# Low parts of the down projections' activation operands: from subtractions on VectorE and GpSimd to adding transfers

## Chip, cores and metric

One core of a Trainium2 chip. The metric is the device time of one execution in microseconds (us); of several executions the median is taken.

## What is computed

Two decoder layers over 1024 tokens of 1024 features, in float32. Each layer is attention (latent attention in layer 0, differential attention in layer 1) and then a SwiGLU block of 2816 hidden columns; a norm ends the program.

```python
def _swiglu(h, w_gate_up, w_down):
    gu = h @ w_gate_up
    return (jax.nn.silu(gu[..., :D_FF]) * gu[..., D_FF:]) @ w_down
...
        h = h + _swiglu(_rmsnorm(h, ffn_norm[l]), ffn_w_gate_up[l], ffn_w_down[l])
    return _rmsnorm(h, final_norm)
```

The change touches the operands of the product with `w_down`, once in each layer.

## The kernel before

**Numbers.** TensorE multiplies float32r operands. A float32 value is split into a high part (rounded to float32r) and a low part (what is left), and a product takes three matmuls: high by high, low by high, high by low (`product`, L1264). `split` (L412) makes such a pair: ScalarE writes the high part with an activation, then VectorE, or GpSimd where `sub` says so, subtracts it from the source and writes the low part.

**The down projection.** `block_tail` (L1126) holds what follows attention. Its first stage (`up`, L1339) makes the gated hidden columns in 11 pairs and writes them to HBM (`act_d`); its second stage (`down`, L1406, and `down_last`, L1440) multiplies them by `w_down` in Strassen's form with seven products. The operands of the seven products come from `stage(p)` (L1529): it loads four tiles of a pair p from `act_d` into tiles named `stg` and makes four sums of them on VectorE; `place(xs, p, i)` (L1550) then splits the staged tile of form i into `xh` and `xl`, 128x512 each. There are 11 pairs of 7 forms in 2 layers, 154 calls of `place`. Forms 0, 1, 3 and 5 are subtracted on VectorE (88 instructions), forms 2, 4 and 6 on GpSimd (66).

```python
    GROUPS = ((0, 1), (2, 3, 4), (5, 6, 7), (8, 9, 10))
    SLOTS = (0, 1, 2, 3, 0, 1, 2, 3, 0, 1, 2)
```

The 11 pairs are multiplied in four groups. For a group, `down` runs over n = 0 to 3, and for each n over the seven products; a product of a group of three pairs is nine matmuls. There are four places (slots) for operands. While group g is multiplied, `prepare` stages and places those pairs of group g + 1 whose slots the group does not use. The other pairs (one of group 1, two each of groups 2 and 3) can be placed only at n = 3, form i right after product i has read the old tile; we call this a group switch. The 14 operands of group 0 are placed while the last pair of `up` runs and right after it.

In the second stage VectorE also subtracts weight columns from each other (`wr`), makes their low parts (`wl`; the high parts `wh` come from ScalarE), and adds each product from PSUM (`pa`, `pb`, `pc`) to the sums `h`. GpSimd has little but the 33 subtractions of each layer.

**The order.** The instructions of a stage are recorded, and a planner (`Plan`) sets their order once, when the program is built: it takes, with costs from `cost` (L294), what can start first on each engine. Each engine then runs its instructions in that order. All recorded instructions are issued in one line, so the profile shows L287 for nearly all of them; tiles tell them apart. SP issues all DMAs. GpSimd issues none.

Of the kernel before, what the change touches and what calls it, by code (L numbers as in the profile page):

```python
# [14 lines left out]
AF = mybir.ActivationFunctionType  # L15
ALU = mybir.AluOpType
# [176 lines left out]
class Plan:  # L193
# [100 lines left out]
    def cost(self, engine, name, n, dtype, psum, accum, size):  # L294

        if engine == "tensor":
            if name == "transpose":
                return 0.107, self.HOP
            return n * (1 if dtype == F32R else 6 if n <= 64 else 8) / 2400, self.HOP
        if engine == "scalar":  # L300
            return (0.05 if psum else 0.09) + n / 1200 + 0.19 * accum, self.HOP
        if engine == "vector":
            return 0.067 + n / 960 + 0.063 * (name == "scalar_tensor_tensor" and not psum), self.HOP
        if engine == "gpsimd":
            return (0.245 + n / 1200 if name == "tensor_scalar" else 0.15 + n / 475), self.HOP
        return max(0.45, size / 360e3), 2.2
# [64 lines left out]
def trunk(ctx: ExitStack, tc: tile.TileContext, A: dict):  # L371
    nc = Plan(tc)
# [33 lines left out]
    def f32(ap):  # L406
        return ap.bitcast(F32)
# [4 lines left out]
    def split(dst_hi, dst_lo, src, scale=1.0, sub=None):  # L412
        nc.scalar.activation(dst_hi, src, AF.Copy, scale=scale)
        if isinstance(scale, float) and scale == 1.0:
            (sub or nc.vector).tensor_tensor(dst_lo, src, f32(dst_hi), ALU.subtract)
        else:
            nc.vector.scalar_tensor_tensor(dst_lo, src, scale, f32(dst_hi), ALU.mult, ALU.subtract)

    def mm3(ps, parts):
        n = len(parts)  # L420
        for i, (lh, ll, rh, rl) in enumerate(parts):
            nc.tensor.matmul(ps, lhsT=lh, rhs=rh, start=i == 0, stop=False)
            nc.tensor.matmul(ps, lhsT=lh, rhs=rl, start=False, stop=False)
            nc.tensor.matmul(ps, lhsT=ll, rhs=rh, start=False, stop=i == n - 1)
# [117 lines left out]
    with tc.using_default_side("right"):  # L542
# [9 lines left out]
                t=("z6", "z7", "z8", "z9", "t", "t"), xh=[q + "h" for q in spare], xl=[q + "l" for q in spare],  # L552
# [76 lines left out]
    for k in range(KT):  # L629
        xt[k] = load_x(0, k)  # L630
        raw = wa_p.tile([P, NA * P], F32, name="war", tag="war", bufs=3)
        wh = wa_p.tile([P, NA * P], F32R, name=f"wah{k}", tag=f"wah{k}")
        wl = wa_p.tile([P, NA * P], F32R, name=f"wal{k}", tag=f"wal{k}")
        cuts = (0, 2 * P, 4 * P, NA * P) if k == 0 else (0, NA * P)
        if k == 0:
            nc.sync.dma_start(out=gains, in_=A["gains"])
        for a, b in zip(cuts, cuts[1:]):
            nc.sync.dma_start(out=raw[:, a:b], in_=A["wa"][k, :, a:b])
            split(wh[:, a:b], wl[:, a:b], raw[:, a:b], sub=nc.vector if k < 2 else nc.gpsimd)
        wa_h.append(wh)  # L640
        wa_l.append(wl)
# [4 lines left out]
    def compressed(f, acc, r):  # L646
# [17 lines left out]
        for norm, (which, _, lo_n, n_t, dst_h, dst_l) in zip(norms, kinds):  # L664
            yield
            rr = norm.spread()
            for n in range(n_t):
                t = tmpa.tile([P, HF], F32, name="cn", tag="t")
                nc.vector.scalar_tensor_tensor(t, raws[lo_n + n], gain(which, n), rr, ALU.mult, ALU.mult)
                split(dst_h[n][f], dst_l[n][f], t)  # L670
# [3 lines left out]
        nc.vector.tensor_tensor(m2[0:64], kraw[64:128], cs[64:128, tok], ALU.mult)  # L674
        nc.vector.tensor_tensor(m1[0:64], m1[0:64], m2[0:64], ALU.add)
        split(krh[0:64, tok], krl[0:64, tok], m1[0:64])
        for t in (krh, krl):
            move(t[64:128, tok], t[0:64, tok])
# [447 lines left out]
    def block_tail(layer, half, resid, last, side_work=None, ahead=None, meanwhile=None):  # L1126
# [11 lines left out]
        def zpool(place):  # L1138
            return z1 if int(place[1:]) < 10 else z2
# [11 lines left out]
        def dtile(i, s):  # L1151
            return xtile(*DOWN.get((i, s), (i, s)))
# [374 lines left out]
        staged = {}  # L1527
# [11 lines left out]
        def prepare(xs, free, pairs):  # L1539

            for p in free:
                yield from stage(p)
                for i in range(7):
                    place(xs, p, i)
                    if i % 2:
                        yield
            for p in pairs:
                yield from stage(p)

        def place(xs, p, i):  # L1550
            t = dtile(i, SLOTS[p])
            split(*t, staged[p][i], sub=nc.vector if i in (0, 1, 3, 5) else nc.gpsimd)
            xs[i].append(t)


# [34 lines left out]
        for p in range(NJ // 2):  # L1590
            if p == 2 and side_work is not None:
                side_work(z1)
            if p == CUT[layer]:
                quarter_operands(1, whole, nc.vector)
            for m, i in ups[p]:
                if p < NJ // 2 - 1:
                    continue
                if (m, i) == (1, 1):
                    for _ in stage(0):
                        pass  # L1600
                    place(xs, 0, 0), place(xs, 0, 1)
                if (m, i) == (0, 4):
                    for _ in stage(1):
                        pass
                if m == 1 and i >= 2:
                    place(xs, 0, i)
# [3 lines left out]
        for g in range(len(GROUPS) - 1):  # L1610
# [5 lines left out]
            for n in range(4):  # L1616
                i = 0
# [362 lines left out]
```

## Time and profile before

| | |
|---|---|
| median of 3 runs | 2520.44 us (2517.12 to 2521.76) |
| the profiled execution | 2517.07 us, of which 2515.0 us are the span of the trace |
| granted TensorE clock, mean | 0.977 of full speed |
| TensorE busy (PE) | 2335.8 us, 93% |
| VectorE busy (DVE) | 1929.2 us, 77% |
| ScalarE busy (ACT) | 1164.3 us, 46% |
| GpSimd busy (POOL) | 1125.1 us, 45% |

PE is TensorE's matmul, PEld its weight load, DVE VectorE, ACT ScalarE, POOL GpSimd, SP the engine that issues DMAs. Busy shares are means over stages that have different limits, so the argument goes by stretches of the span. The `stg` tiles are read by `place` from 933 to 1172 us (layer 0) and from 2204 to 2440 us (layer 1). A matmul's end is modelled and overlaps the next one's start, so how fast TensorE runs is read from starts and counts, not from busy time.

### The profile page before, as it was taken

What the parts mean: (1) busy time and instruction counts of PE and PEld (TensorE: products, weight loads), DVE (VectorE), ACT (ScalarE), POOL (GpSimd) and SP (SyncE); (2) the same over time, 40 slices, a digit from 0 to 9 for tenths busy, and PEclk for the clock granted to TensorE, in tenths of its full rate; (3) what the DMA queues carried; (4) which work ended last, traced back from release to release, by engine and by line L of the source; (5) the groups of instructions that cost most, each with busy time, mean ns of one, the idle gap of its engine ahead of it and who ended that gap; (6) DMA issues with size and microseconds to landing.
All of it is one profiled execution on the core that took longest, in us unless ns stands there. A gap on an engine that the chain in (4) does not pass through costs nothing. (4 is left out here: it accounts for less than half of the span.)

```text
span 2515.0 us, 38090 instructions
## 1 busy us (share of the span) xinstructions
PE 2335.8 (93%) x12744; PEld 1996.4 (79%) x12744; DVE 1929.2 (77%) x3685; ACT 1164.3 (46%) x2319; POOL 1125.1 (45%) x979
## 2 busy tenths in 40 slices
PE   8689999999899998999999999989989999988997
PEld 6579988778788886777788888878768888876777
DVE  6575555387887789999678677676598787789997
ACT  4246555244444444344355555554344444454442
POOL 2145652163555554123377674444264555542212
PEclk9899999999999998999999999999999999999999
DMA  5156665566332235332266663373744232244322
GB/s 182 22 158 203 197 199 177 163 214 202 111 92 72 84 104 179 92 105 92 87 201 198 207 196 113 106 233 125 251 142 154 79 93 72 85 147 149 103 66 73
DMA packets 204691, 347.41 MB, mean 138 GB/s; under 512 B 26832, under 2 KB 59856, under 8 KB 204496
## 3 DMA queue, kind: packets, MB, share of 16 engines
q1 hardware_dynamic: 204496, 344.99, 43.8%
q8 instruction: 101, 1.65, 0.3%
q14 instruction: 94, 0.77, 0.1%
HBM read 240.94 MB, written 95.04 MB: 134 GB/s over the span
## 5 line engine op out<-in xcount | busy, mean ns | idle before, releaser
L287 ACT ACTIVATE wh<-wr 128x512 fp32r<-128x512 f32 (+2 forms) x530 | 287.5, 550 | 450.1 <-PE pb L287 137.7
L287 DVE TENSOR_TENSOR wl<-wr,wh 128x512 fp32r<-128x512 f32 (+2 forms) x530 | 396.0, 761 | 38.6 <-ACT wh L287 38.0
L287 PE MATMUL pa<-xh,wh 128*128 128x512 f32 (+1 forms) x850 | 339.6, 401 | 35.9 <-DVE h L287 16.2
L287 PE MATMUL pa<-xh,wl 128*128 128x512 f32 (+1 forms) x850 | 337.3, 398 | 18.4 <-DVE wl L287 17.1
L287 PE MATMUL pa<-xl,wh 128*128 128x512 f32 (+1 forms) x850 | 336.6, 396 | 4.0 <-DVE xl L287 4.0
L287 PE MATMUL pb<-xh,wh 128*128 128x256 f32 (+1 forms) x976 | 293.7, 304 | 23.4 <-DVE s L287 17.4
L287 PE MATMUL pb<-xl,wh 128*128 128x256 f32 (+1 forms) x976 | 293.0, 301 | 0.0
L287 PE MATMUL pb<-xh,wl 128*128 128x256 f32 (+1 forms) x976 | 291.8, 301 | 0.0
L287 POOL TENSOR_TENSOR wr<-wr 128x512 f32<-128x512 f32 x128 | 179.6, 1403 | 172.6 <-DMA wr<-wgu 84.3
L287 POOL TENSOR_TENSOR xl<-stg,xh 128x512 fp32r<-128x512 f32 x66 | 110.9, 1698 | 305.3 <-ACT xh L287 159.0
L287 PEld LDWEIGHTS pa<-xh,wh 128*128 128x128 f32 x850 | 163.0, 192 | 77.5 <-DVE h L287 14.6
L287 PEld LDWEIGHTS pb<-xh,wh 128*128 128x128 f32 x976 | 187.6, 193 | 46.2 <-DVE s L287 26.6
L287 PEld LDWEIGHTS pa<-xh,wl 128*128 128x128 f32 x850 | 162.1, 191 | 57.0 <-DVE wl L287 24.8
L287 PEld LDWEIGHTS pb<-xl,wh 128*128 128x128 f32 x976 | 188.5, 193 | 13.7
L287 PEld LDWEIGHTS pb<-xh,wl 128*128 128x128 f32 x976 | 188.0, 193 | 6.0 <-DVE wl L287 0.5
L287 PEld LDWEIGHTS pa<-xl,wh 128*128 128x128 f32 x850 | 163.0, 192 | 34.4 <-DVE xl L287 5.7
L287 POOL TENSOR_SCALAR p<-p,tot 128x640 f32<-128x640 f32 (+7 forms) x128 | 98.9, 774 | 180.6 <-DVE tot L287 114.0
L287 ACT ACTIVATE p<-sc,nmax 128x128 f32<-128x128 f32 (+7 forms) x192 | 141.8, 740 | 77.6 <-DVE nmax L287 45.3
L287 POOL TENSOR_TENSOR qt<-wr 128x256 f32<-128x256 f32 x120 | 102.8, 876 | 124.8 <-DVE wl L287 107.2
L287 DVE TENSOR_TENSOR s<-s,pb 128x256 f32<-128x256 f32 (+1 forms) x278 | 115.6, 426 | 39.5 <-PE pb L287 36.6
L287 PE MATMUL pc<-xh,wh 128*128 128x512 f32 x352 | 139.1, 398 | 4.5 <-DVE h L287 4.3
L287 PE MATMUL pc<-xl,wh 128*128 128x512 f32 x352 | 138.9, 395 | 2.5 <-DVE xl L287 2.5
(295 smaller groups left out, 6491.2 us busy)
## 6 DMA issues: line engine op xcount, KB each, us to landing
wr<-wgu SPq DMA_DIRECT2D x142, 256.0 KB, 3.2
act_d<-s SPq DMA_DIRECT2D x88, 256.0 KB, 2.5
stg<-act_d SPq DMA_DIRECT2D x88, 256.0 KB, 2.9
wr<-wd SPq DMA_DIRECT2D x96, 192.0 KB, 2.4
pb<-wgu SPq DMA_DIRECT2D x60, 256.0 KB, 4.0
preh<-ph SPq DMA_DIRECT2D x58, 256.0 KB, 3.0
prel<-pl SPq DMA_DIRECT2D x58, 256.0 KB, 2.8
wh<-preh SPq DMA_DIRECT2D x58, 256.0 KB, 4.8
```

Source lines behind the costliest of these rows:

```text
L287: return getattr(getattr(self.nc, engine), name)(*map(put, args), **{k: put(a) for k, a in kw.items()})
```

## The change

`place` no longer calls `split`. For all seven forms ScalarE writes the high part as before, then writes the negated rounded source, which is the negated high part, into the low tile, and a DMA issued from GpSimd adds the staged tile to the low tile in place. The subtractions on VectorE and GpSimd are gone. The planner gets a cost for such a DMA.

```diff
@@ -301,6 +301,8 @@
             return (0.05 if psum else 0.09) + n / 1200 + 0.19 * accum, self.HOP
         if engine == "vector":
             return 0.067 + n / 960 + 0.063 * (name == "scalar_tensor_tensor" and not psum), self.HOP
+        if name == "dma_start" and engine == "gpsimd":
+            return 0.9, 3.8
         if engine == "gpsimd":
             return (0.245 + n / 1200 if name == "tensor_scalar" else 0.15 + n / 475), self.HOP
         return max(0.45, size / 360e3), 2.2
@@ -416,6 +418,12 @@
         else:
             nc.vector.scalar_tensor_tensor(dst_lo, src, scale, f32(dst_hi), ALU.mult, ALU.subtract)
 
+    def low_by_transfer(dst_hi, dst_lo, src):
+
+        nc.scalar.activation(dst_hi, src, AF.Copy)
+        nc.scalar.activation(dst_lo, src, AF.Copy, scale=-1.0)
+        nc.gpsimd.dma_start(out=f32(dst_lo), in_=src, accum_op=ALU.add)
+
     def mm3(ps, parts):
         n = len(parts)
         for i, (lh, ll, rh, rl) in enumerate(parts):
@@ -1549,7 +1557,10 @@
 
         def place(xs, p, i):
             t = dtile(i, SLOTS[p])
-            split(*t, staged[p][i], sub=nc.vector if i in (0, 1, 3, 5) else nc.gpsimd)
+            if i in (0, 1, 2, 3, 4, 5, 6):
+                low_by_transfer(*t, staged[p][i])
+            else:
+                split(*t, staged[p][i], sub=nc.vector if i in (0, 1, 3, 5) else nc.gpsimd)
             xs[i].append(t)
 
 
```

The planner's order moves with it, at three places that matter here. The first is GpSimd where `up` ends and the second stage begins (`wr` and `qt` are sums of the last gate and up weights, `xl<-stg` the low parts of the operands). Before:

```order
L287 TENSOR_TENSOR qt<-wr,qt 128x256
L287 TENSOR_TENSOR wr<-wr 128x512 x4
L287 TENSOR_TENSOR xl<-stg,xh 128x512
L287 TENSOR_TENSOR qt<-wr 128x256 x2
L287 TENSOR_TENSOR qt<-wr,qt 128x256
L287 TENSOR_TENSOR xl<-stg,xh 128x512
L287 TENSOR_TENSOR qt<-wr,qt 128x256
L287 TENSOR_TENSOR xl<-stg,xh 128x512 x27
```

Now:

```order
L287 DMA xl<-stg 128x512
L287 TENSOR_TENSOR wr<-wr 128x512 x2
L287 DMA xl<-stg 128x512
L287 TENSOR_TENSOR wr<-wr 128x512
L287 DMA xl<-stg 128x512
L287 TENSOR_TENSOR wr<-wr 128x512
L287 DMA xl<-stg 128x512
L287 TENSOR_TENSOR qt<-wr 128x256 x2
L287 DMA xl<-stg 128x512
L287 TENSOR_TENSOR qt<-wr,qt 128x256
L287 DMA xl<-stg 128x512
L287 TENSOR_TENSOR qt<-wr,qt 128x256
```

Six issues of transfers now stand ahead of the last `qt`, where two subtractions stood, and three more `wr` are behind a transfer.

The second is VectorE at a group switch of layer 0 (`h` takes the sums from PSUM, `wr` and `wl` are weight columns of the next n). Before:

```order
L287 TENSOR_TENSOR h<-h,pb 128x512
L287 TENSOR_TENSOR xl<-stg,xh 128x512
L287 TENSOR_TENSOR wl<-wr,wh 128x384
L287 TENSOR_TENSOR h<-h,pa 128x512
L287 TENSOR_TENSOR wr<-wr 128x384
L287 TENSOR_TENSOR xl<-stg,xh 128x512 x2
L287 TENSOR_TENSOR h<-h,pc 128x512
L287 TENSOR_TENSOR xl<-stg,xh 128x512
L287 TENSOR_TENSOR wl<-wr,wh 128x384
L287 TENSOR_TENSOR h<-h,pa 128x512
```

Now:

```order
L287 TENSOR_TENSOR h<-h,pb 128x512
L287 TENSOR_TENSOR h<-h,pa 128x512
L287 TENSOR_TENSOR h<-h,pc 128x512
L287 TENSOR_TENSOR h<-h,pa 128x512
L287 TENSOR_TENSOR h<-h,pc 128x512
L287 TENSOR_TENSOR h<-h,pa 128x512 x2
L287 TENSOR_TENSOR wl<-wr,wh 128x384 x3
```

No operand work stands between two additions from PSUM; the weights' low parts `wl` come later than the sums.

The third is ScalarE at the same switch (`wh` are high parts of weight columns). Before:

```order
L287 ACTIVATE xh<-stg 128x512 x3
L287 ACTIVATE wh<-wr 128x384
L287 ACTIVATE xh<-stg 128x512
L287 ACTIVATE wh<-wr 128x384
L287 ACTIVATE xh<-stg 128x512 x3
L287 ACTIVATE wh<-wr 128x384
L287 ACTIVATE xh<-stg 128x512 x3
```

Now (the pattern of the last two rows goes on, until 27 activations have run without a `wh`):

```order
L287 ACTIVATE wh<-wr 128x384 x22
L287 ACTIVATE xl<-stg 128x512
L287 ACTIVATE xh<-stg 128x512 x2
L287 ACTIVATE xl<-stg 128x512 x2
L287 ACTIVATE xh<-stg 128x512 x2
L287 ACTIVATE xl<-stg 128x512
L287 ACTIVATE xh<-stg 128x512
```

The high and negated parts of the operands have moved together, and the weights' high parts ahead of them and behind them.

## Rows read from the trace of the kernel before

**Rows 1.** The page: busy us, share and count of engines; VectorE in 40 slices.
```profile
PE 2335.8 (93%) x12744; PEld 1996.4 (79%) x12744; DVE 1929.2 (77%) x3685; ACT 1164.3 (46%) x2319; POOL 1125.1 (45%) x979
...
DVE  6575555387887789999678677676598787789997
```
**Rows 2.** Stretches of the second stages: PE, PEld, DVE, ACT, POOL busy; clock, DMA share, GB/s.
```profile
980.00:1010.00 30.00, 24.88 (x96) 18.75 (x95) 30.00 (x56) 12.26 (x25) 9.75 (x6) 0.89 0.70 226
1010.00:1190.00 180.00, 166.29 (x709) 132.42 (x708) 176.71 (x293) 75.96 (x149) 45.38 (x30) 0.99 0.32 97
...
2260.00:2290.00 30.00, 24.66 (x90) 17.80 (x89) 29.97 (x54) 11.43 (x25) 9.82 (x6) 0.89 0.67 221
2290.00:2450.00 160.00, 147.42 (x630) 118.01 (x629) 155.58 (x261) 67.21 (x132) 33.90 (x21) 0.99 0.30 91
```
**Rows 3.** Matmuls in time order, 14 without a wait: start, us.
```profile
1050.01 0.39 PE L287 MATMUL pb<-xh,wh 128*128 128x512 f32 x1
...
1052.96 0.39 PE L287 MATMUL pc<-xh,wh 128*128 128x512 f32 x1
```
**Rows 4.** Whom PE waited for, 980 to 1190: us in total, times, longest.
```profile
PE pa L287 <- DVE h L287: 9.0, 7, 2.3
PE pc L287 <- DVE h L287: 3.6, 2, 3.1
PE pa L287 <- DVE wl L287: 3.2, 1, 3.2
```
**Rows 5.** VectorE's groups, 980 to 1190: busy us, mean ns.
```profile
L287 DVE TENSOR_TENSOR wl<-wr,wh 128x384 fp32r<-128x384 f32 x76 | 47.1, 634 | 0.0
...
L287 DVE TENSOR_TENSOR xl<-stg,xh 128x512 fp32r<-128x512 f32 x34 | 30.9, 921 | 0.0
L287 DVE TENSOR_TENSOR wr<-wr 128x384 f32<-128x384 f32 x47 | 29.5, 636 | 0.0
L287 DVE TENSOR_TENSOR stg<-stg 128x512 f32<-128x512 f32 x36 | 28.6, 801 | 0.0
```
**Rows 6.** VectorE and GpSimd in time order, 1136 to 1165: start, us.
```profile
1139.27 0.55 DVE L287 TENSOR_TENSOR wl<-wr,wh 128x384 fp32r<-128x384 f32 x1
...
1143.86 1.66 DVE L287 TENSOR_TENSOR wl<-wr,wh 128x384 fp32r<-128x384 f32 x1
...
1143.67 3.00 POOL L287 TENSOR_TENSOR xl<-stg,xh 128x512 fp32r<-128x512 f32 x2 [38.08 <-ACT xh L287]
```
**Rows 7.** The tile stg, its readers: duration ns min/median/max; last, its loads' time to landing.
```profile
L287 ACT ACTIVATE xh<-stg x154: 612/628/637, 933.2 to 2437.4; 128x512 fp32r<-128x512 f32 x154
L287 SPq DMA_DIRECT2D stg<-act_d x88: 319/326/1054, 685.0 to 2388.5; - x88
L287 DVE TENSOR_TENSOR xl<-stg,xh x88: 677/686/1786, 934.6 to 2437.5; 128x512 fp32r<-128x512 f32 x88
L287 DVE TENSOR_TENSOR stg<-stg x88: 678/683/1792, 947.9 to 2401.2; 128x512 f32<-128x512 f32 x88
L287 POOL TENSOR_TENSOR xl<-stg,xh x66: 1267/1614/4807, 954.1 to 2439.3; 128x512 fp32r<-128x512 f32 x66
...
DMA to landing us min/median/max: 2.3/2.9/5.0
```
**Rows 8.** In time order where the second stage of layer 0 begins: start, us, idle before.
```profile
954.06 4.81 POOL L287 TENSOR_TENSOR xl<-stg,xh 128x512 fp32r<-128x512 f32 x1 [6.92 <-ACT xh L287]
958.83 1.44 POOL L287 TENSOR_TENSOR qt<-wr 128x256 f32<-128x256 f32 x2
...
960.30 0.63 ACT L287 ACTIVATE wh<-qt 128x512 fp32r<-128x512 f32 x1 [3.74 <-POOL qt L287]
...
967.07 0.58 PE L287 MATMUL pb<-xh,wh 128*128 128x256 f32 x1 [6.15 <-DVE s L287]
```
**Rows 9.** A DMA from SBUF to SBUF (128 KB each): us to landing.
```profile
qa<-qa SPq DMA_DIRECT2D x32, 128.0 KB, 2.7
```

## The prediction, made before the changed kernel ran

> **What bounds the kernel now.** I read the page first: PE 93% busy, VectorE 77% [rows 1]. Taken as means these would say that VectorE's work is hidden. The 40 slices of VectorE show otherwise: four nines from slice 16 (943 to 1195 us) and three from slice 37 (2264 to 2452), where the second stages lie. So I read the stretches next [rows 2]. From 980 to 1190 us VectorE is busy 30.00 of 30 and 176.71 of 180 us, from 2260 to 2450 us 29.97 of 30 and 155.58 of 160. It has no room in either layer.
>
> What PE loses there comes from its pace. Between [rows 3] 13 matmuls start in 1052.96 − 1050.01 = 2.95 us, 0.227 us each. At that pace the 709 matmuls from 1010 to 1190 need 160.9 us of 180: 19 us lost. The 630 from 2290 to 2450 need 143 of 160: 17 lost. The first 30 us of the two stages hold 96 and 90 matmuls, 21.8 and 20.4 us: 8.2 and 9.6 lost. So 36 us are lost in the middles and 18 in the starts, 54 together. Not all can come back, but nothing more can from PE's waits in these stretches.
>
> Who ends the waits: VectorE's additions `h` that free the PSUM tiles, 9.0 and 3.6 us, and its `wl`, 3.2 us in one wait [rows 4]. The starts have a second suspect: DMA share 0.70, and a clock of 0.89 against 0.99 later [rows 2].
>
> VectorE is also slowed. A `wl` takes 0.55 us alone, and 1.66 us when GpSimd subtracts beside it, whose two subtractions take 3.00 us then [rows 6]. Over the stretch the mean of `wl` is 634 ns [rows 5], 84 over the undisturbed one.
>
> **The change part by part.**
>
> *Removed from VectorE:* 88 subtractions [rows 7] at 0.92 us (the mean in the stretch [rows 5]): 81 us, of which 34, 30.9 us, are in 980 to 1190. With GpSimd's subtractions goes the disturbance: 76 `wl` × 84 ns = 6.4 us; 47 `wr`, 636 against some 550 for a like shape, 4.0 us; 36 `stg`, 801 against 683 [rows 5, 7], 4.2 us. VectorE's 206.7 us in layer 0 become about 161, while PE wants (96 + 709) × 0.227 = 183. VectorE is then no longer the bound: 88% of what PE wants. What is late next is a single `wl` or `h` at the wrong moment, or the operands. I take two thirds of the 36 us back, **−24**; the ends are 0 and −36.
>
> *Removed from GpSimd:* 66 subtractions, at least 66 × 1.27 = 84 us [rows 7], on an engine with 45 of 180 us busy [rows 2]. By themselves they are worth nothing, except in one place. At 954.06 one takes 4.81 us, the `qt` behind it starts at 958.83, ScalarE's `wh` had idled 3.74 us for it, and PE had waited 6.15 us when it starts at 967.07 [rows 8]. An issue stands there now, but six of them stand ahead of the last `qt` instead of two subtractions. I take −3.5 in each layer, **−7**; the ends are −12 and 0.
>
> *Added to ScalarE:* 154 activations like the 154 of `xh`, 0.628 us each [rows 7]: 97 us, 48 a layer. ScalarE is busy 88 of 210 us [rows 2]; with some 36 more it is at 60%. Slack in PE's order covers it, except at a group switch. There 14 operands are 28 activations, at 0.53 to 0.63 us 15 to 17.6 us, and product i of n = 3 (nine matmuls, 2.04 us) frees tile i; seven take 14.3 us. ScalarE so keeps up within 3 us, but a `wh` that falls behind the run of 27 waits up to 17 us. The order puts 22 `wh` ahead of the run, which is its cover. If that cover is short PE waits for `wh`. I allow **+5** for the four large switches and the two small ones; the ends are 0 and +12.
>
> *Added to GpSimd:* 154 issues of DMAs. The trace of before has none on this engine. Bounds by the nearest rows: 0.33 us, SP's issue [rows 7], and 4.81 us, the longest held subtraction [rows 8]. I take 1.3 us, the shortest GpSimd instruction on a tile of this size (1.267 [rows 7]), because the work is one pass over 128 rows of descriptors. 14 of a switch take 18 us; they have 14.3 us of product time plus the next group's first products, 12.4 us until the fourth pair of low parts is needed, 26.7 together. So at 1.3 us they are hidden: 0. The point from which they are not is 26.7 / 14 = 1.9 us for the last of a switch, and 2.4 us with the slack of later products.
>
> *Added to the queues:* 154 transfers of 256 KB from SBUF to SBUF. The rows next to it land after 2.3 to 5.0 us, median 2.9 (HBM to SBUF) [rows 7], and 2.7 us for 128 KB from SBUF to SBUF [rows 9]; I take 3, with 5 as the far end, which a switch has room for (an operand made at its product's end is wanted 14 us later). In bandwidth, 226 GB/s at a share of 0.70 [rows 2] are 323 GB/s at full share, so a transfer is 0.8 us of all 16 engines, or 1.6 if the old contents are read as well. In the middle, at a share of 0.32, one in 2.7 us changes nothing. In a start some 14 fall on 9 us of free DMA time: 11 to 22 us. That can delay weights, up to 13 us a start. Against it VectorE is free to make the `stg` sums and the weights earlier. Of the 18 us in the starts I take a third back, **−6**; the ends are −18 and +26.
>
> SP issues nothing more and nothing on SP is passed. In other stages the instructions stay: 0, and nothing hides or uncovers them.
>
> **Sum:** −24 − 7 + 5 − 6 = −32. The profiled execution took 2517.07 us; the median of the runs, 2520.44, is 3.4 above it. 2517.07 − 32 = 2485; beside the runs that is 2488, and I say **2487**.
>
> **A rule against the change.** [Rows 6] show that VectorE and GpSimd hold each other up when both take two operands from SBUF. The Trainium skill, page "SBUF — State Buffer", section "SBUF: two separate sides", tells of a trap: a DMA issued from GpSimd needs that engine to write its descriptors, and it can't while VectorE holds the shared port in a two-port mode; the transfer then looks blocked. Its section "Who interferes with whom" adds that a two-input VectorE operation takes only the read side, and infers that it would not starve the descriptors. By the first, the sum would turn into the first rival's; by the second it stays as above. No row of before shows a GpSimd issue, so none decides.
>
> **Rivals.**
>
> *1. Issues on GpSimd are held by VectorE (slower).* The place is the start of a second stage and each large switch. The price: VectorE is nearly always busy there, and a GpSimd subtraction beside it is stretched from 1.27 to 4.81 us [rows 7]; if an issue is stretched to 3 us, 14 are 42 us against 26.7, 15 lost at each of two large switches, and 17 at the start against some 25 us: 47 a layer, 94 in both. With −36 gained elsewhere it is +58: **2575**. It decides from 2.4 us per issue. For it: rows 6. Against it: an issue reads no operand tile, and VectorE now has gaps. Chance 0.13; milder forms that end just above no change, by operands that land late, another 0.05.
>
> *2. The starts become bound by transfers.* The middle gives its 24, the starts lose 13 to 20 of it back, the block gives a little: about −10, **2510**. For it: DMA share 0.70 and 0.67 [rows 2]. Against it: part of the 14 lie before 980. Chance 0.17.
>
> *3. It moves nothing.* ScalarE takes VectorE's place: `wh` is behind 27 operand activations at a switch, and `h` no longer ends the wait but `wh` does; 36 us of waits keep their size. **2520**. For it: the order. Against it: ScalarE at 60%. Chance 0.08.
>
> *4. Everything comes back.* The 54 us and 12 of the block: 66, less the pipeline's own gaps: **2455**. For it: VectorE falls to 88% of PE's need. Against it: the clock of 0.89 in the starts is no matter of VectorE alone. Chance 0.12.
>
> **How the numbers follow.** Forecast 0.45 (its own range 2472 to 2500), rivals 0.18, 0.17, 0.08 and 0.12. A measurement of this kernel can tell 0.2%, about 5 us. Faster: 0.45 + 0.17 + 0.12 = 0.74. Same: 0.08. Slower: 0.18. The range leaves out the worst of rival 1 and the best of rival 4: 2452 to 2535.
>
> **What would show it.** Right: VectorE's busy time falls by some 110 us (81 and 30) to about 1815, its share in 1010 to 1190 below 95%, `wl` near 550 ns; ScalarE rises to about 1260; PE makes 42 to 44 matmuls in 10 us of the middle instead of 39.4; GpSimd's transfers land in about 3 us after the issue; the 4.81 us block is gone. Wrong: GpSimd's issues 2.4 us apart or more at a switch, PE's waits ended by a DMA into `xl` or by `wh`, or DMA shares of 0.9 at the starts. If `h` still ends PE's waits with VectorE below 90%, the loss in the middle was never a matter of its load but of the order, and the sum's first term falls.

## The result, and the profile after

The changed kernel takes 2542.38 us (median of 4 runs, 2541.92 to 2548.53); the kernel before, beside it, 2520.43 us. The ratio is 1.0095, 95% interval 1.0076 to 1.0113: some 22 us **slower**. The forecast was 2487 us, the range ended at 2535, and the slower side had a chance of 0.18. (In the later runs the kernel before had medians of 2526 to 2528 us, so what follows goes by ratios to the runs beside it: −0.5% is half a per cent faster than before.)

The page after: the busy times, VectorE's slices, the DMA queues and the issues that answer to [rows 1, 7].

```profile
PE 2342.5 (92%) x12744; PEld 2002.8 (79%) x12744; DVE 1834.1 (72%) x3597; ACT 1237.5 (49%) x2473; POOL 1152.0 (45%) x1067
...
DVE  6575555387978785868678677676688778777688
...
q0 software_dynamic: 22176, 40.38, 9.2%
...
L287 POOL DMA_DIRECT2D xl<-stg x154 | 135.5, 892 | 304.8 <-ACT xl L287 173.3
...
xl<-stg POOLq DMA_DIRECT2D x154, 256.0 KB, 5.6
...
stg<-act_d SPq DMA_DIRECT2D x88, 256.0 KB, 4.9
wr<-wd SPq DMA_DIRECT2D x96, 192.0 KB, 3.2
```

VectorE did shed its load: 95 us less, and its nines in the second stages are gone. GpSimd's work didn't shrink: its 154 issues are 135.5 us, more than the 66 subtractions had been. New is the queue q0: 154 transfers, 9.2% of 2540.3 us, which is 1.52 us of all 16 DMA engines for each; the prediction had 0.8, or 1.6 if the old contents are read too. They land after 5.6 us (median; 8.7 at most), and the loads of the staged tiles, 2.9 us before [rows 7], now after 4.9 (10.2 at most).

The stretches of [rows 2], after:

```profile
980.00:1010.00 30.00, 20.29 (x69) 14.14 (x67) 16.52 (x34) 13.56 (x29) 10.29 (x12) 0.83 1.10 291
1010.00:1190.00 180.00, 163.75 (x683) 131.82 (x684) 137.06 (x252) 94.95 (x191) 50.85 (x57) 0.95 0.74 171
...
2260.00:2290.00 30.00, 18.65 (x75) 14.45 (x75) 13.76 (x32) 14.69 (x32) 9.56 (x11) 0.83 1.09 295
2290.00:2450.00 160.00, 140.52 (x578) 112.72 (x577) 118.72 (x226) 78.95 (x160) 38.70 (x45) 0.93 0.74 176
```

VectorE is at 137 of 180 us in the middle where it had 176.71, yet PE makes 683 matmuls there, not 709, and 69 in the start, not 96. The DMA share in the starts reads 1.10 and 1.09, where before had 0.70 and 0.67: the 16 engines have no time left. And the granted clock is lower, 0.95 and 0.93 against 0.99.

**Where the time goes: a chain through the staging tiles.** VectorE in time order, 1040 to 1054 us (start, duration, instruction, idle before):

```profile
1044.70 0.55 DVE L287 TENSOR_TENSOR wl<-wr,wh 128x384 fp32r<-128x384 f32 x1
1050.97 0.69 DVE L287 TENSOR_TENSOR stg<-stg 128x512 f32<-128x512 f32 x1 [5.72 <-issue]
1051.58 0.68 DVE L287 TENSOR_TENSOR h<-h,pa 128x512 f32<-128x512 f32 x1
```

PE, the same stretch:

```profile
1046.58 0.39 PE L287 MATMUL pb<-xl,wh 128*128 128x512 f32 x1
1052.40 0.77 PE L287 MATMUL pa<-xh,wh 128*128 128x512 f32 x1 [5.44 <-DVE h L287]
1052.97 0.63 PE L287 MATMUL pa<-xl,wh 128*128 128x512 f32 x1
1053.40 0.63 PE L287 MATMUL pa<-xh,wl 128*128 128x512 f32 x1
```

And SP's queue in 1040 to 1052, its issues and then whom it waited for (us in total, times, longest):

```profile
1043.04 0.33 SPq L287 DMA_DIRECT2D stg<-act_d  x1
1043.46 1.02 SPq L287 DMA_DIRECT2D wr<-wd  x1
1046.28 0.33 SPq L287 DMA_DIRECT2D stg<-act_d  x1
...
SPq L287 <- DMA xl<-stg: 11.1, 4, 6.8
```

Read from below: a staging tile is reloaded by SP for a later pair. It may be reloaded only when the transfer that reads the old tile has **landed** (before: when a subtraction of 0.9 us was done). SP waits for that, then loads; VectorE stands 5.72 us before the sum of the loaded tiles, and the addition `h`, whose matmuls had run by 1046.5, stands behind the sum in VectorE's order. For this wait the profile names no releaser ("issue"), but the times do: the transfer issued at 1040.76 lands at 1046.27, SP's load is issued at 1046.28 and lands at 1050.89, and the sum starts at 1050.97. PE waits 5.44 us for `h`. Its matmuls then start 0.43 us apart where they started 0.23 apart before the gap; the granted clock is 0.65 from 1050 to 1055 us, so most of that is at the lower of its two levels (1.2 and 2.4 GHz). (By the program's order the sum at 1050.97 is one of pair 6; its tiles alternate with the pairs' numbers, and the load of 1046.28 goes over a tile that pair 4's last transfer reads.) The same happens once more, with pair 8 in the tiles of pair 6, where SP waits up to 8.7 us for a transfer and the profile names the load as the releaser. VectorE and PE there:

```profile
1115.03 0.69 DVE L287 TENSOR_TENSOR stg<-stg 128x512 f32<-128x512 f32 x1 [8.77 <-DMA stg<-act_d]
1115.64 0.68 DVE L287 TENSOR_TENSOR h<-h,pa 128x512 f32<-128x512 f32 x1
```

```profile
1116.38 0.80 PE L287 MATMUL pa<-xh,wh 128*128 128x512 f32 x1 [6.55 <-DVE h L287]
```

Over 980 to 1190 PE's `pa` matmuls wait for `h` 20.0 us in 5 waits; before, 9.0 in 7 [rows 4]. Layer 1 shows the same: 20.1 us in 4 waits from 2260 to 2470, the longest 7.2, and there VectorE waits 18.8 us in 4 for loads of staging tiles.

```profile
PE pa L287 <- DVE h L287: 20.0, 5, 6.5
```

### The profile page after: what moved, and what is told of

The parts are those of the page before. It is cut to its first block, busy times and chain, and to the rows that moved or that the text cites. A ratio compares the mean times of both kernels' runs of the same rounds, so it can differ in the third digit from the quotient of the medians.

```text
span 2540.3 us, 38434 instructions
## 1 busy us (share of the span) xinstructions
PE 2342.5 (92%) x12744; PEld 2002.8 (79%) x12744; DVE 1834.1 (72%) x3597; ACT 1237.5 (49%) x2473; POOL 1152.0 (45%) x1067
## 3 DMA queue, kind: packets, MB, share of 16 engines
q8 instruction: 101, 1.65, 0.3%
## 4 chain that ended last, share of the span: by engine, by line
PE 58%; DVE 19%; DMA 11%; issue 7%; POOL 2%; ACT 2%; SPq 1%; POOLq 0%; DVEq 0%; ACTq 0%
PE pa L287 16%; PE pb L287 10%; PE psp L287 7%; PE pc L287 6%; PE sc L287 5%; DVE wl L287 4%; PE pso L287 3%; PE psv L287 3%; PE pswo L287 3%; DVE s L287 3%; DVE h L287 3%; PE tp L287 2%; DVE xl L287 2%; DMA xl<-stg 2%; DMA rd<-rsy 1%
## 5 line engine op out<-in xcount | busy, mean ns | idle before, releaser
L287 DVE TENSOR_TENSOR wl<-wr,wh 128x512 fp32r<-128x512 f32 (+2 forms) x530 | 374.0, 721 | 47.7 <-ACT wh L287 46.9
L287 PE MATMUL pb<-xh,wh 128*128 128x256 f32 (+1 forms) x976 | 292.2, 303 | 20.1 <-DVE sg L287 13.2
L287 POOL DMA_DIRECT2D xl<-stg x154 | 135.5, 892 | 304.8 <-ACT xl L287 173.3
L287 POOL TENSOR_TENSOR qt<-wr 128x256 f32<-128x256 f32 x120 | 109.2, 930 | 134.1 <-DVE wl L287 112.6
```

The source lines that it names most:

```text
L287: return getattr(getattr(self.nc, engine), name)(*map(put, args), **{k: put(a) for k, a in kw.items()})
```

## The experiments

**Is it the transfers' own time?** Two kernels issue everything as the change does, in the same order on every engine, but add 16 or 64 of 128 rows, so that the other rows' low parts are left out:

```diff
-        nc.gpsimd.dma_start(out=f32(dst_lo), in_=src, accum_op=ALU.add)
+        nc.gpsimd.dma_start(out=f32(dst_lo)[0:16, :], in_=src[0:16, :], accum_op=ALU.add)
```

> Each of the 154 transfers adds 16 of the 128 rows of its tile; the low parts of the other rows stay the negated high part (left out). Order of every engine, ScalarE's two writes and GpSimd's issues stay as in the change; only the transfers' bytes fall to an eighth. Theory A (the transfers' own DMA time: they fill the DMA queues, land after 5.6 us, the staging tiles come free late, their reload and VectorE's sums of them stand ahead of the additions h): landing falls to about 2.5 to 3 us, DMA share at 980 to 1010 to about 0.7, and the time to 2485 to 2505, which is the gain that the prediction saw. Theory B (ScalarE's second write, or the order the planner made, costs the time whatever the transfers move): 2535 to 2545, as with the change. Theory C (issues on GpSimd): also 2535 to 2545, since the issues stay.

> As the run with 16 rows, with 64 rows per transfer (half of the low part is left out). Theory A: between the two, landing 3.5 to 4.5 us and 2500 to 2525. Theories B and C: 2535 to 2545.

16 rows: 0.9789 (0.9768 to 0.9811), −2.1% or 54 us; at 2474.18 us it is faster than the 2485 to 2505 expected. 64 rows: 0.9964 (0.9946 to 0.9981). By the share of q0 a transfer takes 0.32 us of all engines with 16 rows, 1.00 with 64 and 1.52 with 128; the time goes from −2.1% over −0.4% to +0.95%. So theory A holds: the gain is there and is more than the forecast's 32 us, ScalarE's second writes and GpSimd's issues don't stop it, and the transfers' own time takes it all and more. Theories B and C fall. With 64 rows the transfers land after 5.3 us, not the 3.5 to 4.5 expected, and the start is still nearly full (share 0.98 at 980 to 1010); with 16 rows they land after 3.1 us. The stretches with 16 rows:

```profile
980.00:1010.00 30.00, 26.39 (x104) 19.82 (x104) 27.98 (x59) 19.20 (x43) 9.94 (x13) 0.94 0.83 246
1010.00:1190.00 180.00, 178.06 (x788) 145.81 (x787) 153.83 (x279) 100.24 (x198) 53.87 (x62) 1.00 0.43 113
```

788 matmuls in 180 us are 0.228 us each, the pace of [rows 3]: with light transfers nothing is lost in the middle.

**ScalarE alone.** Before, with the second write and the subtraction behind it:

```diff
         nc.scalar.activation(dst_hi, src, AF.Copy, scale=scale)
+        if twice:
+            nc.scalar.activation(dst_lo, src, AF.Copy, scale=-1.0)
```

> The kernel before, with ScalarE's second write of every low tile added and the subtraction kept behind it: no transfer at all. Theory A: ScalarE's 97 us are covered, 2515 to 2530. Theory B (ScalarE's work is the cost): 2535 or more.

0.9965 (0.9953 to 0.9978): no cost. It is even a little faster, though work was only added. The order moves with every instruction, and that may alone be worth a third of a per cent; no smaller difference between kernels of different order shows a cause.

**The order.** The planner took 3.8 us to landing; here 8 (and 1.5 us for an issue instead of 0.9; the two were not tried apart):

```diff
-            return 0.9, 3.8
+            return 1.5, 8.0
```

> The change, with the planner's cost of a transfer set to 1.5 us and 8 us to landing (it was 0.9 and 3.8; the change's trace shows 5.6 median and 10.2 at most), so that the order puts VectorE's sums of reloaded staging tiles behind more additions h. The transfers and their bytes stay. Theory A in the form that the loss is VectorE standing in order before a late sum: 2505 to 2530. In the form that the DMA engines are simply full and weights and operands come late in any order: 2535 to 2550. Theory B: below 2525 if the order alone is at fault.

0.9954 (0.9939 to 0.9968): with the same 154 transfers and bytes, 1.4% (36 us) faster than the change, and faster than before. Its middle, by the same view:

```profile
980.00:1010.00 30.00, 17.34 (x57) 12.58 (x57) 13.90 (x30) 11.00 (x24) 7.71 (x9) 0.80 1.09 298
1010.00:1190.00 180.00, 173.86 (x748) 140.75 (x748) 152.06 (x281) 104.90 (x211) 58.38 (x64) 0.99 0.80 189
```

The middle has 748 matmuls, not 683, at a DMA share of 0.80, higher than the change's 0.74. VectorE's waits there for staged tiles and their loads are 4.0 us in 2 for loads and 1.6 in one for a transfer, where the change has 9.5 in 2 and one of 5.7. The start is as bad as in the change. So in the middle it was the order, made for transfers that land early, that lost; in the start it is something else.

**Which pairs.** The start pairs (0, 1), the free pairs (2, 3, 5, 8), which `prepare` places ahead of time, and the switch pairs (4, 6, 7, 9, 10), alone by transfer with the change's costs:

```diff
-            if i in (0, 1, 2, 3, 4, 5, 6):
+            if p in (4, 6, 7, 9, 10):
```

> Transfers only for the 14 operands of group 0 (pairs 0 and 1) in each layer, 28 in all; the other 126 low parts are subtracted as before. Theory A (transfers cost DMA time, so they cost most where the queues were already full): the start stretches hold fewer matmuls than before (about 70 in place of 96 at 980 to 1010), the middles stay as before; 10 to 20 us slower than the kernel before. Rival (the loss is at the group switches): 0 to 5 us faster.

> Transfers only for the five pairs placed at group switches (4, 6, 7, 9, 10), 70 in all. Theory A: VectorE loses 40 subtractions, but the late staging tiles at the switches cost gaps of 5 to 7 us each before an h: between 10 us faster and 10 us slower than before. Rival (the loss is all in the starts): 15 to 30 us faster.

> Transfers only for the four pairs (2, 3, 5, 8) that are placed while nothing waits for them, 56 in all. Theory A: the queues have room for most of them (share 0.32 before in the middle), VectorE loses 32 subtractions: 8 to 20 us faster than before. Rival (any transfer delays the loads of weights): the same time as before or slower.

Then by twos, and all but pairs 2 and 3:

> Transfers for pairs 0, 1 and 2, 3, 5, 8 (start and free), subtractions at the switches; 84 transfers. Alone, these two gave -0.24% and -0.29%. Theory D (the loss of the whole change comes where free and switch pairs both go by transfer, because the switch pair's staging tiles are then released by a late transfer): they add up, -0.4 to -0.6%, 2511 to 2517 for a before of 2526. Theory E (28 transfers of the start and of pairs 2 and 3 crowd the first 110 us of the stage, which no part alone did): 0 to +1%.

> Transfers for pairs 0, 1 and 4, 6, 7, 9, 10 (start and switch), 98. Theories D and E alike: the two gains add up, about -0.9%, 2498 to 2508. A third theory (the cost just goes with the number of transfers, as in the series of 16, 64 and 128 rows): -0.1 to +0.3%.

> Transfers for pairs 2 to 10 (free and switch), 126. Theory D: the gains of the parts (-0.29% and -0.65%) are lost, with gaps of 5 to 7 us before an h at the switches as in the whole change: -0.2 to +0.8%. Theory E: they add up, -0.8 to -1.0%.

> Transfers for all pairs but 2 and 3, 126 in all. Theory E: the start is no longer crowded, and the time is -0.5 to -1.0% against before. Theory D: the gaps at the switches stay, since pairs 5 and 8 still go by transfer ahead of 7 and 10: -0.2 to +0.8%.

| by transfer | ratio − 1 | sum of the parts |
|---|---|---|
| start | −0.24% (−0.37 to −0.11) | |
| free | −0.29% (−0.42 to −0.16) | |
| switch | −0.65% (−0.89 to −0.41) | |
| start, free | +0.10% (−0.04 to +0.23) | −0.53% |
| start, switch | −0.58% (−0.73 to −0.44) | −0.89% |
| free, switch | +0.38% (+0.25 to +0.50) | −0.94% |
| all but 2, 3 | +0.43% (+0.29 to +0.57) | |
| all | +0.95% (+0.76 to +1.13) | −1.18% |

The expectation for the start pairs alone (10 to 20 us slower) missed; the rival's 0 to 5 us faster came out. Matmuls at 980 to 1010 did fall to 69, but 930 to 980 had 296 where before had 234: GpSimd's long subtraction [rows 8] is gone, and that pays for it. The other two missed as well: the free pairs gained 6 us, not 8 to 20, and the switch pairs 17, which is in the range of a rival (the loss is all in the starts) that the start pairs' run speaks against. Start and switch together missed both forecasts (−0.9%, and −0.1 to +0.3%).

Each part is faster alone, though start and free by less than the third of a per cent that an order may be worth. The loss lies in pairs of parts: free with switch +1.32% over their sum, start with free +0.63; start with switch, +0.31, is no more than an order's worth. The single effects and these three make +1.08%, which the intervals leave uncertain by 0.4; the whole change has +0.95. Free with switch is theory D's place: its gaps come back (PE waits 5.25 us for an `h` until 1060.99), and all but 2 and 3 still pays for it (5.30 us until 1053.16). But the switch pairs alone have such a late sum too, one in each layer (VectorE waits 5.2 and 5.6 us); with the free pairs beside them layer 1 has 18.2 us in 4. Which tile is late is as told above, that of the pair two before; that the free pairs' own tiles are the late ones, as the expectation had it, was not shown. Start with free is theory E: pairs 2 and 3 are staged while the transfers of pairs 0 and 1 still fill the queues, 28 transfers, 43 us of all DMA engines. Theory E's forecast for the run without 2 and 3 missed; D is the larger.

**Order or full queues.** The sets again with the longer cost, and the change with the longer cost and 16 rows for pairs 0 to 3:

```diff
-                low_by_transfer(*t, staged[p][i])
+                low_by_transfer(*t, staged[p][i], 16 if p < 4 else P)
```

> Pairs 2 to 10 by transfer, as in the run that was 0.38% slower than before, with the planner's cost 1.5 and 8 us. Theory F (order: the planner took landing for 3.8 us, so VectorE stands before a late sum with h behind it): the gaps at 1047 to 1053 and 1110 to 1116 go, and the time is 0.7 to 1.2% below before. Theory G (the queues are full where free and switch pairs both go by transfer): within 0.3% of the run with the old cost, +0.1 to +0.7%.

> The five switch pairs by transfer, which gave -0.65%, with the longer cost. Theory F: no late sum was in the way there, so nothing is gained, -0.4 to -0.9%. Theory G: the same.

> Start and switch pairs by transfer, which gave -0.58%, with the longer cost. Theory F: the part of +0.31% by which the two fell short of their sum comes back, -0.8 to -1.1%. Theory G: -0.4 to -0.7%.

> All pairs by transfer with the longer cost (-0.46% with whole transfers), but for pairs 0 to 3 the transfers add 16 of 128 rows (the other rows' low parts stay the negated high part). Order and issues stay. If the starts lose by the transfers' DMA time: 980 to 1010 holds about 100 matmuls in place of 57, DMA share falls below 0.9 there, and the time is 1.0 to 1.7% below before. If the starts lose by the order or by the loads of the sums h from HBM alone: -0.3 to -0.7%.

Free and switch: 0.996 (0.9946 to 0.9974), from +0.38 to −0.40%. The two gaps named are gone, yet the gain is between the theories: the order is 0.8 of the 1.3%, and the rest stays. Its start is still full, by the free pairs 2 and 3:

```profile
980.00:1010.00 30.00, 20.75 (x87) 15.46 (x87) 21.09 (x43) 18.64 (x39) 11.59 (x12) 0.86 1.06 297
```

Switch alone: 0.9921 (0.9903 to 0.9938), 2507.07 us beside 2526.97: the lowest ratio of a kernel **with the whole computation**, clearly below the kernel before and the change, though not clear of the same pairs with the old cost (0.9935), whose late sums are gone here. Start and switch: 0.9935 (0.9918 to 0.9952), theory G's −0.4 to −0.7%; theory F's part does not come back. Light transfers for pairs 0 to 3: 0.9826 (0.9808 to 0.9843), 1.3% faster than with whole ones in the same order on every engine, and its start has 106 matmuls, at a clock of 1.00:

```profile
980.00:1010.00 30.00, 26.20 (x106) 18.57 (x105) 26.10 (x54) 19.09 (x42) 10.46 (x14) 1.00 0.86 247
```

So the starts lose by the transfers' time in the queues.

**Fewer transfers for the same relief.** Only VectorE's forms, longer cost:

```diff
+            if p >= 2 and i in (0, 1, 3, 5):
```

> Pairs 2 to 10, forms 0, 1, 3 and 5 alone by transfer (72), GpSimd subtracts the other three, longer cost in the planner. If a transfer is worth VectorE's relief less its DMA time: 0.7 to 1.2% below before (126 transfers with the same relief gave -0.40%). If GpSimd's remaining subtractions, beside its issues and VectorE, take that back: 0.1 to 0.5% below.

> The five switch pairs, forms 0, 1, 3 and 5 alone by transfer (40), longer cost. By the first view 0.7 to 1.2% below before (70 transfers gave -0.79%); by the second 0.2 to 0.6%.

> Transfers for forms 0, 1, 3 and 5 (all 88 subtractions of VectorE), while GpSimd keeps its 66 subtractions. VectorE gets the whole relief, the queues 88 of the 154 transfers. Theory A (cost goes by DMA time): between the change and the run with 64 rows, 2505 to 2525. Rival (GpSimd's subtraction hold up its issues and VectorE): 2530 or more.

All three are worse than hoped. Pairs 2 to 10: 1.0019 (1.0001 to 1.0036), slower than both views had it. Switch pairs: 0.998 (0.9967 to 0.9993), at the near end of the second view. All pairs with the old cost: 0.9987 (0.9971 to 1.0003), 2525.49 us, just past theory A's 2525 and short of the rival's 2530. So fewer transfers with VectorE's own subtractions gone did not give the same relief. VectorE's group `wl` from 980 to 1190 us, in the run of pairs 2 to 10 and in the run of free and switch pairs with all forms:

```profile
L287 DVE TENSOR_TENSOR wl<-wr,wh 128x384 fp32r<-128x384 f32 x75 | 51.7, 711 | 2.8 <-ACT wh L287 2.8
```

```profile
L287 DVE TENSOR_TENSOR wl<-wr,wh 128x384 fp32r<-128x384 f32 x73 | 43.5, 618 | 0.9 <-ACT wh L287 0.9
```

With GpSimd's subtractions staying, `wl` takes 711 ns in the mean, worse than the 634 of [rows 5]; in the change it is 565. The trace of the first shows where: the 53 `wl` with nothing of GpSimd beside them take 0.55 us, the 9 beside an issue 0.55, the 9 beside a subtraction 1.65. So the relief came from GpSimd's subtractions going as well, not from VectorE's own alone. What an order of its own adds to these three was not separated.

## Why the prediction was wrong

**The step that failed** is "Added to the queues". It asked when a transfer lands, and who waits for the low part: "I take 3, with 5 as the far end, which a switch has room for (an operand made at its product's end is wanted 14 us later)". PE does have that room: in layer 0 it waited 2.1 us in all for a transfer into `xl`. But the transfer also *reads* a staging tile, and whoever reloads that tile waits for the landing. The working named no one behind the source of the transfer, though the order of VectorE with its `stg` and `h` was there to read. The price of 3 us was off as well: 5.6 median, 8.7 at most (the 10.2 of an expectation above is the longest load of a staging tile), since the 3 came from loads in the less busy queues of before.

Also in that step, "in the middle … one in 2.7 us changes nothing" held for the bytes (0.80 share with the longer cost, 748 matmuls) and not for the order, which is made once with a landing of 3.8 us. That cost in the diff was never set against the measured 2.9 for a load and what the added traffic does to it. And "in a start some 14 fall on 9 us" left out pairs 2 and 3, which make it 28 from 930 to 1010. That is rival 2, and its 13 to 20 us for the starts were about right, as the table below shows; what it had wrong is that the middle would still give its 24.

**The sum, term by term.** Windows of fixed time hold other work in a faster kernel. Counted instead by the same matmuls (those that before ran in the window, by their number in PE's order), the stretches changed by so many us against before, both layers together, in one profiled execution of each kernel, so that a few us tell nothing:

| | forecast | the change | 16 rows | longer cost | longer cost, 16 rows for pairs 0 to 3 |
|---|---|---|---|---|---|
| block (930 to 980, 2200 to 2260) | −7 | −6.0 | −19.4 | −15.5 | −16.4 |
| starts (980 to 1010, 2260 to 2290) | −6 | +18.5 | −6.4 | +21.2 | −9.9 |
| middles (1010 to 1190, 2290 to 2450) | −24 | +9.0 | −31.3 | −24.4 | −26.4 |

- VectorE's relief, −24, in the middles: it is there with light transfers (−31.3, within the stated ends) and with the longer cost; in the change it turned into +9.0, by the chain above. VectorE's busy time fell by 95 us, not by 110.
- The block on GpSimd, −7: right. The other three runs gain more there; in the change a new wait of 5.8 us for `sg`, a tile of the first stage, stands in layer 0.
- The starts, −6: +18.5. This and the middles are what "Added to the queues" had wrong.
- ScalarE, +5: it is covered; the run with only its writes added was not slower.
- Issues on GpSimd, 0, at 1.3 us each: 0.86 us median and 1.38 at most. The reason given for 1.3, a pass over 128 rows, doesn't hold: an issue for 16 rows takes 0.76. Rival 1 (held by VectorE) falls. The trace agrees with what the Trainium skill, page "SBUF — State Buffer", section "Who interferes with whom", infers: no issue in the change is stretched by VectorE's two-input operations the way a subtraction was, to 4.81 us [rows 7]. Of its 154 issues 131 ran beside a VectorE operation of two inputs, at 0.87 us in the median, and 23 beside none, at 0.86. What a two-port mode would do was not tried.
- Rival 3 falls: PE's waits for `wh` are 2.6 us in layer 0 and 3.7 in layer 1.
- Not in the sum: each gap costs more than itself, as PE runs on at the lower clock behind it (0.43 us apart, not 0.23).

From light to whole transfers 3.1% went, some 78 us. Two causes, each by a pair of runs: the order about 36 us (all transfers, the planner's two costs changed), of which the table has 33 in the middles; the bytes of pairs 0 to 3 about 32 us (longer cost, whole against 16 rows), of which it has 31 in the starts. About 10 are left, which no run names; that the two simply add is assumed.

## What to carry to other kernels

Work that is moved from an engine to a DMA is released later on both sides: ask who waits for its result, and also who waits to overwrite its source, and what stands behind that one in each engine's fixed order. A planner's latency for a transfer is part of the change: with a longer cost, 8 us for landings of 5.6 median, the same transfers went from 0.95% slower to 0.46% faster. And fewer can be more: five pairs in eleven gave 0.79%, all eleven 0.46%, with the same costs.

## What had not been expected of the hardware

An adding transfer's time doesn't fall in proportion to its rows: 1.52, 1.00 and 0.32 us of all 16 engines for 128, 64 and 16 rows of 2 KB. The 1.52 is not the full queues' doing: where only the switch pairs go by transfer, at a DMA share of 0.63 in the middle of layer 0, it is 1.58. An issue on GpSimd stays at 0.84 to 1.38 us beside a busy VectorE, and a `wl` beside it at 0.55. And taking half of the VectorE–GpSimd clash away is not half the gain: with VectorE's subtractions gone and GpSimd's left, `wl` became slower (711 and 776 ns) than with both.
